# A decoder layer in fp32 on one core: last stage's second and third part in a written order, the up projection's products in a new order, and changed seams

## The chip, the cores and the metric

The kernel runs on one core of a Trainium2 chip. The metric is the device time of one execution in microseconds, the median of several runs. The engines are named as in the profile: PE (TensorE matmul), PEld (its weight load), DVE (VectorE), ACT (ScalarE), POOL (GpSimd) and SP (SyncE, which issues nearly all DMAs). L184 is line 184 of the kernel before.

## The reference

One decoder layer on x (1024 tokens, 1024 features, float32), with 256 memory tokens:

```python
h = rmsnorm(x, ln1);  z = h @ w_in              # mLSTM and attention inputs, and gates
ml_out = mlstm(...)                             # 4 heads of 128, chunkwise, normed and gated
fx_out = forgetting_attention(...)              # 8 heads of 64, causal, with decay
x = x + concat([ml_out, fx_out]) @ w_out
x = x + cross_attention(rmsnorm(x, ln_x), rmsnorm(mem, ln_mem), w_xq, w_xkv, w_xo)
u = relu(rmsnorm(x, ln2) @ w_ff1)               # 1024 -> 4096
x = x + (u * u) @ w_ff2                         # 4096 -> 1024
return rmsnorm(x, ln_f)
```

## The kernel before

Activations lie feature by token: 128 features on the partitions, eight such tiles (KT), and two halves of 512 tokens (TH). A float32 product is done as three products of rounded parts: `split` (L129 to L136) makes the rounded part `hi` on ACT and the remainder `lo` on DVE, and `mm3` (L182 to L186) issues lo x hi, hi x lo and hi x hi into one PSUM bank. TensorE thus runs on operands that ACT and DVE have to cut beforehand.

The stages in the order of the span: loading and cutting of x and the values' weights with the first products (0 to 50 us), the mLSTM projections and heads (to 380), forgetting attention (to 600), output projection `out_proj` (to 700), cross attention (to 885), the up projection (to 1215), the down projection (to 1510) and the last eighth of it with the final norm (to 1548).

What runs first on an engine is chosen by a scheduler that works on the recorded instructions, except inside `with in_order()`, where each compute engine keeps the order in which the instructions were written. DMAs from SP go in the order of SP's queue, and a DMA that has to wait holds those behind it.

PSUM has eight banks under five names (sc 3, tp 2, mm 1, m2 1, ov 1). A tile of a name can be written again once its earlier contents have been read. SBUF tiles rotate in the same way; `w2("d")` has two buffers, `rotate("d", "e")` alternates over two names with two buffers each.

*Start.* SP loads `vec` (gains, biases), then for each k a piece of x and of the weights, and at k = 2 the gate weights. `cut_w`, `cut_x`, `cut_gates` make the parts; the first matmul needs one of each.

*Memory.* `mem_prepare` loads the memory tokens, sums their squares, and cuts them to DRAM; it is issued after the first stage's last sum.

*Forgetting attention.* `Tile` scores a block of 128 queries against its keys in pieces of up to 512 columns (`parts`); a last piece narrower than 256 is computed 256 wide.

*Output projection.* `out_unit` adds one tile of the product to x for its first part, with x loaded into `rotate("p", "a")`; `full_sink` (L1071) completes it, cuts it for the cross attention and adds its square to `acc`; `row_second` turns the sums into factors.

*Up projection.* The 4096 hidden features are made in 16 pairs, each a 2x2 block product in the Winograd form of Strassen: seven products (jobs) of 12 matmuls instead of eight. Three PSUM banks hold a pair: a takes jobs 1 and 2, c takes 5 and 3, b takes 6, 7 and 4. Between two jobs on a bank the first result has to be read: `p1` (job 1) is copied by ACT, jobs 5 and 6 are added to it by DVE (`add`, L1326), and the final blocks are squared by ACT (`squared`). `jobs` sets the order:

```python
        jobs += [(p_, 1)] + ([(p_ - 1, 4)] if p_ > 2 else []) + [(p_, i) for i in (5, 2, 6, 3, 7)]
```

`left_up` cuts the weights of a pair in three groups, some additions on POOL. `put` cuts a block of the result and stores both parts to DRAM (`right`), from where the down projection loads them; `put_right` returns the steps that combine and store a pair's blocks, one of which is taken ahead of each job. `stretch` multiplies one piece of the residual by the norm's row: load, multiplication and store.

*Last stage.* The rest of the down projection (four k) comes in three parts of columns: 512 tokens of the first half, then 256 and 256 of the second. For each of eight tiles n: 12 matmuls into a bank, DVE adds the residual (L1579), ACT squares it and DVE adds the squares, ACT scales by the gain (L1584). `finish` makes the row of factors: sums by matmuls (L232), `rsqrt_cols` (DVE, POOL's pow at L202, three times DVE), `spread` (L211) of the factors over the partitions into a bank, a copy to `row` (L1558), and then four multiplications by it on DVE (L1563) with a store each (L1564). For the last part DVE reads the factors from the bank. The steps of a part's `finish` are taken between the tiles of the next part.

Of the kernel before, what the change touches and what calls it, by code (L numbers as in the profile page):

```python
# [44 lines left out]
def hybrid_layer(ctx: ExitStack, tc: tile.TileContext, a: dict, out: bass.AP):  # L45
# [146 lines left out]
    def rsqrt_cols(out_, sums, scale, n, over=None):  # L192

        var = col("var", n)
        if over is None:
            v.tensor_scalar(out=var, in0=sums, scalar1=scale, scalar2=EPS, op0=ALU.mult, op1=ALU.add)
        else:
            e = col("t", n)
            v.scalar_tensor_tensor(out=e, in0=over, scalar=EPS, in1=over, op0=ALU.mult, op1=ALU.mult)
            v.scalar_tensor_tensor(out=var, in0=sums, scalar=scale, in1=e, op0=ALU.mult, op1=ALU.add)  # L200
        y = col("y", n)
        g.tensor_tensor(out=y, in0=var, in1=half[:, :n], op=ALU.pow)  # L202
        t = col("t", n)
        v.tensor_tensor(out=t, in0=y, in1=y, op=ALU.mult)
        v.scalar_tensor_tensor(out=t, in0=t, scalar=-0.5, in1=var, op0=ALU.mult, op1=ALU.mult)
        v.scalar_tensor_tensor(out=out_, in0=t, scalar=1.5, in1=y, op0=ALU.add, op1=ALU.mult)

# [18 lines left out]
    def rsqrt_sums(acc, r, nt, parts=1, bank=None, over=None):  # L226

        ps = (bank or ov_)()
        for t in range(nt):
            for e in range(parts):  # L230
                at = (e * nt + t) * P
                nc.tensor.matmul(ps[:, t : t + 1], acc[:, at : at + P], ones, start=e == 0, stop=e == parts - 1)  # L232
        rsqrt_cols(r, ps[:, :nt], 1.0 / D, nt, over)

    def rsqrt_row(acc, r, nt, parts=1, bank=None, over=None):

        rsqrt_sums(acc, r, nt, parts, bank, over)
        rb = (bank or ov_)()
        spread(rb, r, nt)
        return rb[:, : nt * P]  # L240
# [29 lines left out]
    load(vec, a["vec"])  # L270
# [9 lines left out]
    def mem_prepare():  # L280
        acc = w2("b")
        for i in range(KT // 2):
            raw = w2("f")
            load(raw.rearrange("p (k c) -> p k c", k=2), a["mem"][:, 2 * i : 2 * i + 2])
            square_sum(acc, raw, i == 0)
            hi = w2("p", dt=F32R)
            for e in range(2):
                c = slice(e * NM, e * NM + NM)
                gain = vec[:, VEC["ln_mem"] + 2 * i + e :][:, 0:1]
                split(hi[:, c], raw[:, c].bitcast(F32R), raw[:, c], gain)  # L290
            for p_, t in enumerate((hi.bitcast(F32), raw)):
                load(hmd[:, p_, 2 * i : 2 * i + 2], t.rearrange("p (k c) -> p k c", k=2))
        rsqrt_sums(acc, rcol_m, 2, 2)
        to_row(row_m, rcol_m, 2, rowd[1:2, :NM])

# [41 lines left out]
    def cut_x(hf, k):  # L337
        split(h[hf][0][:, k], h[hf][1][:, k], xs[hf][k], vec[:, VEC["ln1"] + k :][:, 0:1])
# [168 lines left out]
    def carried(hd, y):  # L507
# [6 lines left out]
        kt = mm()  # L514
# [155 lines left out]
    with tc.issue_after(last_sum.ins):  # L670
        mem_prepare()
# [391 lines left out]
    for hf in range(2):  # L1063
# [3 lines left out]
        def full_sink(n, hf, ps):  # L1067
# [9 lines left out]
            square_sum(acc, t, n == 0, add=g)  # L1077
            if hf == 1 and n == KT - 3:
                mix_done.append(done)
            if hf and n == 2:  # L1080
                row_second(0, acc0)

        def row_second(hf, acc):
            c = rcol[:, 4 * hf : 4 * hf + 4]
            rsqrt_sums(acc, c, 4)
            at = slice(hf * TH, hf * TH + TH)
            to_row(row[:, at], c, 4, rowd[2:3, at])
# [97 lines left out]
    def left_up(p_, group):  # L1185
# [6 lines left out]
        split(hi, lo, (r1, r2, r1)[group])  # L1192
        if group == 0:
# [4 lines left out]
            by = g if p_ > 1 else v  # L1198
            by.tensor_tensor(out=x21, in0=x21, in1=x22, op=ALU.add)
            sub(x22, x21, x11, by)  # L1200
            sub(x12, x12, x22, by)
            sub(x11, h22.bitcast(F32), x22, by)
            by.tensor_tensor(out=x11, in0=x11, in1=l22.bitcast(F32), op=ALU.add)
        for e in range(2):
            cuts[p_, ((1, 2), (5, 6), (7, 3))[group][e]] = both((hi, lo), lambda t: t[:, e * TH : e * TH + TH].rearrange("p (k c) -> p k c", k=4))
# [3 lines left out]
    raws = {}  # L1209
# [4 lines left out]
    for p_ in range(2, NP - 2):  # L1214
# [54 lines left out]
    for hf in range(2):  # L1269
        oh, ol = act(), act()  # L1270
        for hd in range(XH):
# [7 lines left out]
            if hd == hf == 0:  # L1279
                row_second(1, acc0)  # L1280
# [36 lines left out]

    class Pair:


        def __init__(self, p_):
            self.p_ = p_
            self.u = {}
# [4 lines left out]
        def run(self, i, l):  # L1328
# [8 lines left out]
            if i == 1:  # L1337
                self.p1 = w2("p") if 1 < self.p_ < NP - 2 else row[:, TH * (self.p_ % 2) :][:, :TH]
# [4 lines left out]
            elif i == 5:  # L1343
                t = w4()
                u["22"], self.t1 = t[:, :TH], t[:, TH:]
# [16 lines left out]
    def put(dst, x):  # L1362

        hi = rotate("d", "e").bitcast(F32R)
# [4 lines left out]
    def put_right(b, k, pair):  # L1369

        u11, u12, u21, u22 = (pair.u[c] for c in ("11", "12", "21", "22"))
        t1 = pair.t1
        to = lambda c: [right[b][ORDER.index(c), :, p_, k] for p_ in range(2)]
        t = {}
# [12 lines left out]
        def four():  # L1387
            sub(t[4], t[2], u21)
            put(to("22"), u22)

        return [one, two, lambda: put(to("t3"), u12), four, lambda: put(to("21"), u21), lambda: put(to("t2"), t[2]), lambda: put(to("t4"), t[4])]
# [40 lines left out]

    pairs = {}
    later = []
    for at, (p_, i) in enumerate(jobs):
# [14 lines left out]
        if later:  # L1450
            later.pop(0)()
        pair = pairs.setdefault(p_, Pair(p_))
        pair.run(i, cuts.pop((p_, i)))
        if i == 4:
            b, k = todo[p_][:2]
            later += put_right(b, k, pair) if b < NB - 1 else put_plain(k, pair)
# [96 lines left out]
    def finish(acc, hf, c0, wid, parts, last):  # L1553

        rb = rsqrt_row(acc, col("r", wid // P), wid // P, parts, bank, inv[:, 4 * hf + c0 // P :][:, : wid // P])
        if not last:
            at_ = row[:, hf * TH + c0 : hf * TH + c0 + wid]
            s.activation(at_, rb, AF.Copy)  # L1558
            rb = at_
        yield  # L1560
        for k in range(0, KT, 2):
            y = x2[k // 4][:, k // 2 % 2, :, hf, c0 : c0 + wid]
            v.tensor_tensor(out=y, in0=y, in1=rb.rearrange("p (o c) -> p o c", o=1).broadcast_to([P, 2, wid]), op=ALU.mult)  # L1563
# [4 lines left out]
    for hf, c0, c1 in ((0, 0, TH), (1, 0, 256), (1, 256, TH)):  # L1568
        wid = c1 - c0
        parts = 1 if wid == TH else 2  # L1570
        acc = w2("b")
        for n in range(KT):
            if n // 2 not in w:
                last_weights(n // 2)
            ps = bank()[:, :wid]
# [3 lines left out]
            v.tensor_tensor(out=y, in0=ps, in1=y, op=ALU.add)  # L1579
            if n == KT - 1 and parts == 2:  # L1580
                s.activation(acc[:, wid:], y, AF.Square)
# [3 lines left out]
            if n:  # L1585
                next(ending, None)
        ending = finish(acc, hf, c0, wid, parts, c1 == TH and hf)
    for _ in ending:
        pass
# [54 lines left out]
```

## Time and profile before

| | us |
|---|---|
| median of 3 runs (1546.37 to 1550.0) | 1548.31 |
| profiled execution, its own time | 1549.03 |
| its span | 1547.3 |
| PE busy | 1510.3 |
| DVE busy | 1100.9 |
| ACT busy | 718.8 |
| POOL busy | 483.4 |

The span is the time from the first to the last instruction of the profiled execution; some 1.7 us lie around it. Busy times are sums over instructions. Matmuls overlap in the pipeline, so one of 512 columns shows about 0.39 us although the next starts 0.23 us after it. A wait in the profile is the idle time of an engine ahead of an instruction, put down to the instruction that released it last.

### The profile page before, as it was taken

The page shows a single profiled execution, that of the slowest core. Times are in us where ns is not written, and L with a number is a line of the kernel's source. Part 1 is how long each engine was busy: PE and PEld are TensorE (multiplying, and loading weights), DVE is VectorE, ACT ScalarE, POOL GpSimd, SP SyncE. Part 2 cuts the span into 40 slices and gives each one's busy share as a digit, 9 for nine tenths or more (in the row PEclk, how much of TensorE's full clock was granted, in tenths as well). Part 3 has the DMA queues.
Part 4 walks back from the last instruction along what each step waited for, and adds up shares of the span by engine and source line. Part 5 has one row for each costly group of instructions (what it writes and reads, how often), then busy time and mean ns, then how long its engine had stood idle before and what let it go on. Part 6 is the DMA issues. An engine that isn't in the chain of part 4 may idle for free.

```text
span 1547.3 us, 21934 instructions
## 1 busy us (share of the span) xinstructions
PE 1510.3 (98%) x7729; PEld 1261.5 (82%) x7729; DVE 1100.9 (71%) x1722; ACT 718.8 (46%) x1337; POOL 483.4 (31%) x515
## 2 busy tenths in 40 slices
PE   8999999999999999999999999999999999999997
PEld 8878888889898887788888788777778778888887
DVE  7656676665788874854457987777777787777766
ACT  7324343334678763543344456555455532222234
POOL 0002130413455441511110034453444644433310
PEclk9999999999999999999999999999999999999998
DMA  6422223436887948953344446776776965556623
GB/s 220 122 79 82 100 100 114 130 130 162 253 248 219 305 166 286 327 176 124 122 147 153 150 148 230 268 253 230 250 243 219 370 251 217 219 207 227 236 92 110
DMA packets 118075, 297.25 MB, mean 192 GB/s; under 512 B 13118, under 2 KB 27768, under 8 KB 111820
## 3 DMA queue, kind: packets, MB, share of 16 engines
q1 hardware_dynamic: 117964, 295.84, 55.9%
q8 instruction: 61, 1.00, 0.3%
q14 instruction: 50, 0.41, 0.1%
HBM read 199.08 MB, written 96.71 MB: 191 GB/s over the span
## 4 chain that ended last, share of the span: by engine, by line
PE 82%; DMA 7%; DVE 6%; issue 2%; ACT 2%; POOL 0%; SPq 0%; DVEq 0%; POOLq 0%; ACTq 0%
PE tp L184 7%; PE tp L186 7%; PE tp L185 7%; PE mm L184 5%; PE sc L184 5%; PE sc L186 5%; PE sc L185 5%; PE mm L186 5%; PE mm L185 5%; PE m L184 5%; PE m L186 5%; PE m L185 5%; PE ov L184 2%; PE ov L185 2%; PE ov L186 2%
## 5 line engine op out<-in xcount | busy, mean ns | idle before, releaser
L184 PE MATMUL tp<-act,wl 128*128 128x512 f32 (+1 forms) x448 | 176.1, 394 | 4.8 <-DVE r_f L1326 3.4
L185 PE MATMUL tp<-act,wh 128*128 128x512 f32 (+1 forms) x448 | 175.3, 391 | 0.0
L186 PE MATMUL tp<-act,wh 128*128 128x512 f32 (+1 forms) x448 | 174.9, 392 | 0.0
L133 DVE TENSOR_TENSOR wl<-wr,wh 128x1024 fp32r<-128x1024 f32 (+2 forms) x99 | 126.3, 1276 | 26.7 <-ACT wh L132 26.3
L132 ACT ACTIVATE wh<-wr 128x1024 fp32r<-128x1024 f32 (+2 forms) x99 | 99.0, 1000 | 94.5 <-PE tp L186 32.7
L184 PE MATMUL mm<-act,wl 128*128 128x512 f32 (+1 forms) x336 | 130.6, 389 | 3.5 <-DVE r_e L1071 1.3
L186 PE MATMUL mm<-act,wh 128*128 128x512 f32 (+1 forms) x336 | 129.0, 384 | 0.0
L185 PE MATMUL mm<-act,wh 128*128 128x512 f32 (+1 forms) x336 | 128.8, 383 | 0.0
L184 PE MATMUL m<-act,wl 128*128 128x512 f32 (+1 forms) x312 | 120.3, 386 | 0.9 <-DVE r_a L916 0.9
L186 PE MATMUL m<-act,wh 128*128 128x512 f32 (+1 forms) x312 | 119.3, 382 | 0.0
L185 PE MATMUL m<-act,wh 128*128 128x512 f32 (+1 forms) x312 | 119.1, 382 | 0.0
L184 PEld LDWEIGHTS tp<-act,wl 128*128 128x128 f32 x448 | 84.2, 188 | 25.4 <-DVE r_f L1326 3.8
L184 PE MATMUL sc<-act,wl 128*128 128x512 f32 (+1 forms) x252 | 98.7, 392 | 3.8 <-DVE r_f L1326 2.3
L1410 POOL TENSOR_TENSOR z<-wr 128x256 f32<-128x256 f32 x56 | 53.5, 976 | 150.4 <-DMA wr<-w_ff2q 127.9
L186 PEld LDWEIGHTS tp<-act,wh 128*128 128x128 f32 x448 | 84.2, 188 | 19.2
L185 PEld LDWEIGHTS tp<-act,wh 128*128 128x128 f32 x448 | 84.2, 188 | 18.8
L185 PE MATMUL sc<-act,wh 128*128 128x512 f32 (+1 forms) x252 | 98.4, 390 | 0.0
L186 PE MATMUL sc<-act,wh 128*128 128x512 f32 (+1 forms) x252 | 98.3, 391 | 0.0
L132 ACT ACTIVATE w<-wr 128x768 fp32r<-128x768 f32 (+2 forms) x31 | 25.5, 824 | 127.3 <-PE tp L186 70.3
L132 ACT ACTIVATE wh<-z 128x1024 fp32r<-128x1024 f32 (+1 forms) x54 | 55.5, 1027 | 61.1 <-POOL z L1410 27.3
L133 DVE TENSOR_TENSOR wl<-z,wh 128x1024 fp32r<-128x1024 f32 (+1 forms) x54 | 73.1, 1353 | 12.4 <-ACT wh L132 12.3
L184 PEld LDWEIGHTS mm<-act,wl 128*128 128x128 f32 x336 | 63.3, 188 | 17.2 <-DVE wl L133 2.1
(676 smaller groups left out, 4236.8 us busy)
## 6 DMA issues: line engine op xcount, KB each, us to landing
act<-right SPq DMA_DIRECT2D x35, 1024.0 KB
right<-w SPq DMA_DIRECT2D x56, 256.0 KB
wr<-w_ff2q SPq DMA_DIRECT2D x28, 512.0 KB
act<-fqk SPq DMA_DIRECT2D x48, 256.0 KB
wr<-w_in SPq DMA_DIRECT2D x20, 512.0 KB
wr<-w_ff SPq DMA_DIRECT2D x20, 512.0 KB
right<-r_e SPq DMA_DIRECT2D x35, 256.0 KB
right<-r_d SPq DMA_DIRECT2D x35, 256.0 KB
```

Source lines behind the costliest of these rows:

```text
L132: s.activation(hi, src, AF.Copy)
L133: return v.tensor_tensor(out=lo, in0=src, in1=hi.bitcast(F32), op=ALU.subtract)
L184: nc.tensor.matmul(ps, w[1], x[0], start=first, stop=False, skip_group_check=more)
L185: nc.tensor.matmul(ps, w[0], x[1], start=False, stop=False, skip_group_check=more)
L186: nc.tensor.matmul(ps, w[0], x[0], start=False, stop=last, skip_group_check=more)
L1410: g.tensor_tensor(out=o, in0=x, in1=y, op=op)
```

## The change

The same products are computed; only score products of 640-column rows change in shape.

- Start: `vec` and the gate weights are loaded from ACT's queue after the first piece of x; the gates are cut ahead of x, and the first piece of x in two halves.
- Memory: `mem_prepare` yields between its pieces and is stepped among the mLSTM heads. The transposed keys of head 0 use bank ov.
- Forgetting attention: rows of 640 columns are scored as 384 + 256.
- Output projection: x rotates over five tags, squares are added on DVE, and sums and row transposition are two tiles apart; the second half's follow after heads 0 and 1 of the cross attention.
- Up projection: the jobs come as 1, 5, 6, 2, (4 of the pair before), 3, 7. The third group of weights keeps one sum in a buffer of its own and is cut in two halves. `put` uses the two buffers of "d" alone. Storing is spread over a pair (four steps after job 7, three after job 4). `stretch` loads at one job and multiplies one job later, and then pauses for six.
- Last stage: parts 2 and 3 are inside `in_order()`; `finish` is divided into sums, refinement and spreading, its banks are always ov, and the products' banks rotate over the other seven; the factors are read from PSUM, but for the last part, which also copies them to `row` for POOL's multiplication; the squares of tiles 1 to 5 are added on POOL.

```diff
-        if k == 2:
-            load(wg_raw, a["w_gate"])
...
         load_x(0, k)
+        if k == 0:
+            s.dma_start(vec, a["vec"])
+            s.dma_start(wg_raw, a["w_gate"])
...
-            cut_x(0, k)
             if k in (0, 2, 4):
                 cut_gates(k // 2)
+            cut_x(0, k, 1 if k else 2)
...
-        kt = mm()
+        kt = mm() if hd else ov_()
...
-    with tc.issue_after(last_sum.ins):
-        mem_prepare()
+    closing = mem_prepare()
...
-            self.parts = [(c0, min(c0 + TH, self.wid)) for c0 in range(0, self.wid, TH)]
+            step = 384 if self.wid == 640 else TH
+            self.parts = [(c0, min(c0 + step, self.wid)) for c0 in range(0, self.wid, step)]
...
-            x = rotate("p", "a")
+            x = rotate("p", "b", "a", "p", "b")
...
-            square_sum(acc, t, n == 0, add=g)
+            square_sum(acc, t, n == 0)
...
-        split(hi, lo, (r1, r2, r1)[group])
+        if group < 2:
+            split(hi, lo, (r1, r2)[group])
+        else:
+            for c, x in ((slice(0, TH), x12), (slice(TH, 2 * TH), thirds.pop(p_))):
+                split(hi[:, c], lo[:, c], x)
...
+            s3 = thirds[p_] = w2("e") if p_ > 1 else x11
+            sub(s3, x11, x21, by)
             by.tensor_tensor(out=x21, in0=x21, in1=x22, op=ALU.add)
-            sub(x22, x21, x11, by)
+            sub(x22, x22, s3, by)
             sub(x12, x12, x22, by)
-            sub(x11, h22.bitcast(F32), x22, by)
-            by.tensor_tensor(out=x11, in0=x11, in1=l22.bitcast(F32), op=ALU.add)
...
-        jobs += [(p_, 1)] + ([(p_ - 1, 4)] if p_ > 2 else []) + [(p_, i) for i in (5, 2, 6, 3, 7)]
-    jobs += [(NP - 2, 1), (NP - 3, 4)] + both_of(NP - 2)[1:]
+        jobs += [(p_, i) for i in (1, 5, 6, 2)] + ([(p_ - 1, 4)] if p_ > 2 else []) + [(p_, 3), (p_, 7)]
+    jobs += [(NP - 1, 1), (NP - 1, 6), (NP - 2, 4)] + [(NP - 1, i) for i in (5, 7, 2, 3, 4)]
...
-        hi = rotate("d", "e").bitcast(F32R)
+        hi = w2("d", dt=F32R)
...
-        return [one, two, lambda: put(to("t3"), u12), four, lambda: put(to("21"), u21), lambda: put(to("t2"), t[2]), lambda: put(to("t4"), t[4])]
+        if last:
+            return [four, lambda: put(to("t2"), t[2]), lambda: put(to("t4"), t[4])]
+        return [one, two, lambda: put(to("t3"), u12), lambda: put(to("22"), u22)]
...
-        if at > 30 and at % 4 == 0 and stretches:
+        if at > 31 and at % 8 in (0, 7) and stretches:
             stretch(stretches[0])
-            if at % 8 == 4:
+            if at % 8 == 7:
                 stretches.pop(0)
...
+        nt = wid // P
+        r = col("r", nt)
+        end = rsqrt_sums(acc, r, nt, parts, ov_, inv[:, 4 * hf + c0 // P :][:, :nt], rsqrt_guess)
         yield
+        end()
+        yield
+        rb = ov_()[:, :wid]
+        spread(rb, r, nt)
+        rb2 = rb
+        if last:
+            rb2 = row[:, :wid]
+            s.activation(rb2, rb, AF.Copy)
         for k in range(0, KT, 2):
             y = x2[k // 4][:, k // 2 % 2, :, hf, c0 : c0 + wid]
-            v.tensor_tensor(out=y, in0=y, in1=rb.rearrange("p (o c) -> p o c", o=1).broadcast_to([P, 2, wid]), op=ALU.mult)
+            by, f = (g, rb2) if last and k == 2 else (v, rb)
+            by.tensor_tensor(out=y, in0=y, in1=f.rearrange("p (o c) -> p o c", o=1).broadcast_to([P, 2, wid]), op=ALU.mult)
             load(out[:, k : k + 2, hf * TH + c0 : hf * TH + c0 + wid], y)
             yield
...
-            ps = bank()[:, :wid]
+            turn[0] += 1
+            ps = ps_tile(tags[turn[0] % 7])[:, :wid]
...
+            if n > 1:
+                next(ending, None)
...
-                square_sum(acc[:, :wid], y, n == 0)
+                square_sum(acc[:, :wid], y, n == 0, add=g if at and n < 6 else v)
...
+    part(0, 0, 0, TH)
+    with in_order():
+        part(1, 1, 0, 256)
+        part(2, 1, 256, TH)
+        for _ in ending:
+            pass
```

More of the change, by code (lines that the diff above doesn't have):

```diff
@@ L189, in both, with rsqrt_guess @@
         return f(pair[0]), f(pair[1])
-    def rsqrt_cols(out_, sums, scale, n, over=None):
+    def rsqrt_guess(out_, sums, scale, n, over=None):
         var = col("var", n)
@@ L224, in square_sum, with rsqrt_sums @@
             add.tensor_tensor(out=acc, in0=sq, in1=acc, op=ALU.add)
-    def rsqrt_sums(acc, r, nt, parts=1, bank=None, over=None):
+    def rsqrt_sums(acc, r, nt, parts=1, bank=None, over=None, how=rsqrt_cols):
         ps = (bank or ov_)()
@@ L232, in rsqrt_sums @@
                 nc.tensor.matmul(ps[:, t : t + 1], acc[:, at : at + P], ones, start=e == 0, stop=e == parts - 1)
[L233 to L240, printed above, removed]
+        return how(r, ps[:, :nt], 1.0 / D, nt, over)
     rowd = dram.tile([4, T], F32, name="rowd")
@@ L335, in hybrid_layer, with cut_x @@
     tiles = [[ps_tile(t)[:, :WV] for t in ts] for ts in (("mm", "tp", "m2", "tp"), ("sc", "sc", "sc"))]
-    def cut_x(hf, k):
-        split(h[hf][0][:, k], h[hf][1][:, k], xs[hf][k], vec[:, VEC["ln1"] + k :][:, 0:1])
+    def cut_x(hf, k, n=1):
+        for c in range(0, TH, TH // n):
+            c = slice(c, c + TH // n)
+            split(h[hf][0][:, k, c], h[hf][1][:, k, c], xs[hf][k][:, c], vec[:, VEC["ln1"] + k :][:, 0:1])
     def first_values(hf, k, ts):
@@ L1449, in hybrid_layer @@
             lefts = left(a["w_ff2q"][0, 0])
-        if later:
-            later.pop(0)()
+        for _ in range(2 if len(later) > 5 else 1):
+            if later:
+                later.pop(0)()
         pair = pairs.setdefault(p_, Pair(p_))
         pair.run(i, cuts.pop((p_, i)))
+        b, k = todo[p_][:2]
+        if i in (7, 4) and b < NB - 1:
+            later += put_right(b, k, pair, i == 4)
+        elif i == 4:
+            later += put_plain(k, pair)
         if i == 4:
-            b, k = todo[p_][:2]
-            later += put_right(b, k, pair) if b < NB - 1 else put_plain(k, pair)
             del pairs[p_]
@@ L1567, in hybrid_layer, with part @@
     ending = iter(())
-    for hf, c0, c1 in ((0, 0, TH), (1, 0, 256), (1, 256, TH)):
+    tags = [t for t in cycle if t != "ov"]
+    def part(at, hf, c0, c1):
+        nonlocal ending
         wid = c1 - c0
-        parts = 1 if wid == TH else 2
+        parts = 2 if at else 1
         acc = w2("b")
```

66 lines of the change are left out of this document (35 added, 31 removed).

## The prediction

> **What bounds the kernel now.** I read the page's head first, then the windows by stage, then the waits of TensorE, and for each long wait the timeline around it.
>
> ```profile
> span 1547.3 us, 21934 instructions
> PE 1510.3 (98%) x7729; PEld 1261.5 (82%) x7729; DVE 1100.9 (71%) x1722; ACT 718.8 (46%) x1337; POOL 483.4 (31%) x515
> ...
> 885.00:1215.00 330.00, 318.77 (x1357) 254.34 (x1356) 255.75 (x292) 187.63 (x291) 150.47 (x96) 0.99 0.67 234
> 50.00:380.00 330.00, 329.06 (x1782) 280.69 (x1781) 213.17 (x343) 121.43 (x211) 66.36 (x81) 1.00 0.35 109
> 380.00:600.00 220.00, 216.78 (x1435) 188.93 (x1434) 173.29 (x416) 154.84 (x422) 98.98 (x156) 1.00 0.78 242
> 600.00:700.00 100.00, 96.28 (x459) 78.40 (x457) 64.26 (x82) 46.45 (x80) 30.93 (x24) 1.00 0.73 254
> 1215.00:1510.00 295.00, 294.79 (x1265) 237.25 (x1264) 218.99 (x284) 79.63 (x92) 113.41 (x116) 1.00 0.57 219
> ```
>
> The columns of a window after its length are busy us of PE, PEld, DVE, ACT and POOL. TensorE is busy for 1510.3 of 1547.3 us. The change removes no product, so all it can win, apart from some narrower score products below, is among the 37 us in which TensorE stands still. They are not spread evenly: 330.00 - 318.77 = 11.2 us lie in the up projection (885 to 1215), 3.7 in the output projection (600 to 700), 3.2 in the forgetting attention (380 to 600), 0.2 in the down projection, and most of the rest at the start, at the seam of the first stages, and at the end. What TensorE waited for says which edits can reach them:
>
> ```profile
> PE mm L184 <- DVE wl L133: 8.3, 3, 7.1
> PE tp L184 <- DVE r_f L1326: 3.4, 1, 3.4
> PE mm L211 <- DVE c_r L206: 2.9, 1, 2.9
> PE sc L184 <- DVE r_f L1326: 2.3, 1, 2.3
> PE ov L184 <- DVE r_f L1326: 2.2, 1, 2.2
> PE sc L184 <- DVE wl L133: 1.4, 1, 1.4
> PE mm L184 <- DVE r_e L1071: 1.3, 1, 1.3
> PE mm L184 <- DVE r_c L518: 0.9, 1, 0.9
> ...
> PE m L184 <- DVE act L136: 0.8, 1, 0.8
> ```
>
> The numbers are us in total, times, longest. L1326 is the addition that empties a bank in the up projection; the three waits for it make 7.9 of the 11.2 us there.
>
> **Up projection.** The timeline around the longest of them (start, duration):
>
> ```profile
> 996.66 0.40 PE L185 MATMUL m<-act,wh 128*128 128x512 f32 x1
> 996.89 0.39 PE L186 MATMUL m<-act,wh 128*128 128x512 f32 x1
> 1000.65 0.50 PE L184 MATMUL tp<-act,wl 128*128 128x512 f32 x1 [3.37 <-DVE r_f L1326]
> ...
> 994.26 1.23 DVE L1430 TENSOR_TENSOR w<-w,row 128x1024 f32<-128x1024 f32 x1 [1.55 <-DMA w<-x2d]
> ...
> 998.70 0.69 DVE L133 TENSOR_TENSOR r_p<-r_p,r_d 128x512 fp32r<-128x512 f32 x1
> ...
> 999.91 0.69 DVE L1326 TENSOR_TENSOR r_f<-tp,r_p 128x512 f32<-128x512 f32 x1
> ```
>
> Matmuls of 512 columns issue 0.23 us apart, so a job of 12 is 2.8 us. Bank b takes job 6, is read by the addition, then takes jobs 7 and 4. In the old order 1, 4 (of the pair before), 5, 2, 6, 3, 7 one job lies between 6 and 7, and one between 7 and 4: VectorE has 2.8 us to get to the addition. Here its queue was late by 1.55 us at the multiplication by the row, which waited for its load, and the addition began at 999.91. In the new order 1, 5, 6, 2, 4, 3, 7 the built program has three jobs between 6 and 7, four between 7 and 4 and two between 1 and 2, the shortest: no wait on a bank nearer than 25 matmuls after the first pairs, 5.8 us. The largest lateness seen, 2.8 + 3.37 us, would exceed that by 0.4. So the 7.9 us go. The load for the row's multiplication gets over two jobs instead of standing directly ahead of it, and the waits on wl (1.4, and 1.0 of the 8.3 above) come 25 instead of 23 matmuls after their cause; I count them as gone, -2.4. The remaining 0.9 us, at the first pairs, stay. POOL and VectorE do one operation fewer per pair for the third group; POOL, with 150 of 330 us busy, is no bound, nor is VectorE with 256.
>
> Against it stands the new `put`, which has two buffers for the first half instead of four:
>
> ```profile
> 968.10 6.67 DMA right<-r_e
> ...
> 1014.50 3.20 DMA right<-r_d
> ...
> 95.25 0.63 ACT L132 ACTIVATE r_d<-r_c 128x512 fp32r<-128x512 f32 x1 [4.38 <-DVE r_c L518]
> ```
>
> ScalarE now waits for a store to land, and behind that in its queue stand the activations and the copy of job 1's bank. I leave 1.0 us for it: -7.9 - 2.4 + 1.0 = **-9.3** (from -5.2, half of what goes, to -10.3).
>
> **Start.** Rows of the first 7 us:
>
> ```profile
> 0.79 0.40 SPq L270 DMA_DIRECT2D vec<-vec  x1
> ...
> 5.42 0.72 ACT L135 ACTIVATE act<-act,vec 128x512 fp32r<-128x512 f32 x1 [0.40 <-DMA act<-x]
> 6.17 0.75 DVE L136 SCALAR_TENSOR_TENSOR act<-act,vec,act 128x512 fp32r<-128x512 f32 x1 [0.69 <-ACT act L135]
> 6.48 0.24 ACT L132 ACTIVATE wh<-z 128x48 fp32r<-128x48 f32 x1 [0.34 <-DMA z<-w_gate]
> ```
>
> The vector and the gate weights go to ScalarE's queue, so SP's first weight load leaves 0.4 us earlier, and the first split is cut into halves: the first matmul waits for half of 0.72 + 0.75, another 0.7 less. The gate's split now stands ahead of it, and its landing, 6.48 in the old order, must come forward with its issue; where it doesn't, only some 0.4 is won. Take **-1.0** (-0.4 to -1.4).
>
> **Seams of the first stages.** The memory's squares and splits leave the stretch at 44 to 47 us, where they stood in ScalarE's queue ahead of the values' split that TensorE waited for 0.8 us; they are issued in steps among the mLSTM heads, where TensorE loses 0.9 of 330 us and VectorE is busy 213: that hides them, with their loads, the stores on SP, two sums and a transposition; without that cover they would cost the same 0.8. Head 0's transposed keys go to bank ov, so that the next product no longer waits for their reading (0.9). Sum -1.7 at best; **-1.6** (0 to -1.7).
>
> **Forgetting attention.** Rows of 640 columns are scored as 384 + 256 instead of 512 + 128, where 128 was computed 256 wide: 16 products (8 heads by 2) lose 128 columns, 16 x 0.23 / 4 = -0.9. Of the 3.2 us of stalls around them 0.6 may go with the smaller first piece: **-1.5** (-0.3 to -2.9).
>
> **Output projection.** A rotation of five tags for x instead of two, squares added on VectorE instead of POOL, and the factors' sum and transposition two tiles apart. The waits on L1071 (1.3) and on the other half's addition stand in the 3.7 us; the wait on `r_d` stays at 14 matmuls, as short as before. **-2.0** (+0.5 to -3.5): VectorE, 64 of 100 us busy, takes the additions.
>
> **The end.** Start, duration of the last steps:
>
> ```profile
> 1534.68 0.28 PE L186 MATMUL ov<-act,w 128*128 128x256 f32 x1
> ...
> 1535.44 0.38 ACT L1558 ACTIVATE row<-mm 128x256 f32<-128x256 f32 x1 [0.39 <-PE mm L211]
> ...
> 1535.86 2.50 DVE L1563 TENSOR_TENSOR act<-act,row 128x512 f32<-128x512 f32 x4 [0.44 <-ACT row L1558]
> ...
> 1536.18 0.83 PE L232 MATMUL sc<-ones,r_b 128*128 128x1 f32 x6 [0.66 <-ACT r_b L1581]
> 1538.27 0.16 DVE L200 SCALAR_TENSOR_TENSOR c_var<-sc,c_t 128x2 f32<-128x2 f32 x1
> ...
> 1539.94 1.19 PE L211 MATMUL mm<-ident,c_r 128*128 128x128 f32 x4 [2.93 <-DVE c_r L206]
> 1541.17 2.48 DVE L1563 TENSOR_TENSOR act<-act,mm 128x512 f32<-128x512 f32 x4 [1.38 <-PE mm L211]
> 1541.93 2.12 SPq L1564 DMA_DIRECT2D out<-act  x4
> ...
> L1503 POOL TENSOR_TENSOR act<-act 128x512 f32<-128x512 f32 x12 | 18.1, 1519 | 18.1 <-DVE act L1530 18.0
> ```
>
> The sums ended at 1536.18 + 0.83 = 1537.0, 2.3 us after the last product, but four multiplications of part 2 (2.50 us) kept VectorE from the variance until 1538.27, 3.6 after it. In the written order part 2's scaling is stepped while part 3's products run, and the copy of its row (0.38) no longer stands ahead of the last square; the sums get bank ov only when part 2's last reading is done, for which I add 0.1: variance at 2.3 - 0.4 + 0.1 = 2.05, 1.5 us earlier. Behind the spread matmuls, which ended at 1541.13, it gives some back. Four multiplications of 0.62 ended 2.5 us after that, each with a store behind it. Now the factors are first copied to `row` (0.4), and POOL takes the second multiplication, 1.52 us where VectorE takes 0.62; SP issues the stores in order, 0.53 each, so that two wait behind POOL's: 0.4 + 1.5 + 2 x 0.53 = 3.0 to the last issue. Net -1.5 + 0.5 = **-1.0** (+0.5 to -1.5). [...]
>
> **Sum.** -9.3 - 1.0 - 1.6 - 1.5 - 2.0 - 1.0 = -16.4. The profiled execution took 1549.03 us (span 1547.3 and 1.7 around it); 1549.03 - 16.4 = 1532.6. It lies 0.7 above the median of the runs shown, 1548.31, so the median after is forecast at 1532.
>
> **Rivals.** *Half of the up projection only.* VectorE still works in bursts: the addition at 999.91 was preceded by four of its own operations without a gap, and the new order brings jobs 5 and 6, both of which end in additions to the same copy of job 1, next to each other. If stalls come back at the new places for half the gain, -5.2 stands for -9.3, and the median is 1536; with the smaller terms at their weak ends (-0.4, 0, -0.3, +0.5, +0.5) 1543. For it: 7.9 us sat on three places only, so bursts decide. Against: 25 matmuls are double the old room. 0.20.
>
> *Stores hold ScalarE (slower).* Place: the copy of job 1's bank, which stands behind the first-half copies of `put`. From the end of the job whose result is stored: addition 0.69, three activations of 0.63 and issue make 2.9; landing 3.20 gives 6.1; seven activations of 0.63 to the end of the copy give 10.5. The built order needs the copy 61 matmuls after that job, 14.2 us. So 3.6 us are spare, and a landing of 6.8 uses them up; one of 6.67 was seen. It turns the sign when the mean lateness in the 12 pairs that store this way exceeds 16.4 / 12 = 1.4 us, at landings of 8.2; at 9.2, 12 x 2.4 - 16.4 = +12, some 1561. For it: SP issues in order, and its stores queue behind other waits. Against: the window moves 234 GB/s at a DMA share of 0.67. [...]
>
> *Nothing comes of it.* The stages outside the written order are placed by a scheduler; if its new order moves the stalls rather than removing them, and the end gives back what it wins, the time is 1548. 0.04. The forecast has 0.68.
>
> **Chances.** This kernel's measurement can tell about 0.2%, 3 us, from no change. Faster 0.68 + 0.20 = 0.88, same 0.03, slower 0.09. The range: all terms at their strong ends give -21.3, 1527, and 2 us of spread between runs, 1525; the high end is the weak case, 1543, with the same spread, 1545. The slower rival and no change lie outside.
>
> **What would show it.** In the changed profile: TensorE busy in the up projection to within 2 us of its stage, no wait there on the addition's line over 1 us; the first matmul near 6.1; no wait at 47 and 95 us; the variance 2 us after the last product and the last store's issue 3 us after the spread. The forecast is wrong if ScalarE shows waits for DMA right<-r_d in the up projection with TensorE waits on the copy of job 1 behind them, or if the row's multiplication still waits on its load.

## The result and the profile after

The changed kernel takes 1527.39 us (median of 4 runs, 1526.16 to 1528.97), the kernel before, run again beside it, 1547.58 (4 runs): a ratio of 0.9862 with a 95% interval from 0.9850 to 0.9875, or 20.2 us less. Forecast was 1532, -16.4 us. Two executions far above all others, 2484.25 us at a granted clock of 0.555 (the run with the old schedule of the row's multiplication) and 3549.69 us (the kernel before), count in no median or ratio of this text. The head of the page after, and its windows, cut where the stages begin (columns as in the prediction: length, busy us of PE, PEld, DVE, ACT, POOL, then granted clock, DMA share, GB/s):

```profile
span 1525.5 us, 21947 instructions
PE 1504.9 (99%) x7729; PEld 1261.5 (83%) x7729; DVE 1103.9 (72%) x1740; ACT 722.6 (47%) x1353; POOL 444.7 (29%) x498
...
0.00:48.30 48.30, 41.78 (x325) 41.57 (x326) 35.50 (x73) 33.13 (x59) 5.06 (x14) 1.00 0.59 210
48.30:376.90 328.60, 328.60 (x1785) 280.94 (x1783) 213.97 (x340) 121.78 (x211) 67.64 (x79) 1.00 0.36 111
376.90:694.80 317.90, 313.26 (x1897) 268.01 (x1896) 239.75 (x517) 202.86 (x507) 105.19 (x168) 1.00 0.76 247
...
880.60:1196.10 315.50, 315.50 (x1358) 254.53 (x1357) 257.60 (x307) 191.00 (x307) 125.11 (x87) 1.00 0.68 244
1196.10:1489.60 293.50, 293.50 (x1265) 236.93 (x1264) 221.62 (x283) 76.35 (x88) 114.81 (x112) 1.00 0.58 220
1489.60:1525.50 35.90, 26.46 (x222) 25.93 (x220) 18.75 (x45) 16.12 (x35) 10.99 (x14) 0.87 0.33 118
```

The same stages of the kernel before, cut at the same matmuls:

```profile
0.00:50.00 50.00, 42.13 (x324) 41.96 (x325) 36.10 (x73) 34.53 (x62) 4.21 (x14) 1.00 0.62 214
50.00:380.40 330.40, 329.45 (x1784) 281.09 (x1783) 213.40 (x343) 121.81 (x212) 66.36 (x81) 1.00 0.35 109
380.40:700.90 320.50, 313.55 (x1895) 267.83 (x1895) 237.68 (x499) 201.41 (x502) 129.91 (x180) 1.00 0.76 245
...
886.70:1217.20 330.50, 319.27 (x1359) 254.71 (x1359) 255.26 (x292) 188.38 (x293) 150.47 (x96) 0.99 0.68 236
1217.20:1511.20 294.00, 293.79 (x1266) 236.70 (x1265) 218.47 (x284) 77.91 (x89) 113.41 (x116) 1.00 0.57 217
1511.20:1547.30 36.10, 26.34 (x222) 25.91 (x220) 22.81 (x55) 14.91 (x36) 2.52 (x3) 0.87 0.33 118
```

(The cross attention, 185.80 us in both, is left out.) The lengths of the stages give the account: 1.7 us at the start, 1.8 in the mLSTM heads, 2.6 in forgetting attention and output projection, 0 in the cross attention, 15.0 in the up projection, 0.5 in the down projection, 0.2 in the last stage. Sum 21.8, the difference of the spans. The up projection's TensorE is busy for 315.50 of 315.50 us: no idle time is left there. VectorE and ScalarE do as much as before in less time. What TensorE still waits for:

```profile
PE mm L184 <- DVE act L136: 6.5, 1, 6.5
PE ov L217 <- DVE c_r L209: 1.7, 1, 1.7
PE tp L185 <- DMA act<-mix: 1.3, 1, 1.3
PE ov L238 <- DVE c_t L199: 1.2, 1, 1.2
```

All three waits on the addition are gone, and those at 47 and 95 us. The end of the changed kernel, start and duration:

```profile
1513.56 0.28 PE L186 MATMUL tp<-act,w 128*128 128x256 f32 x1
...
1515.05 1.02 PE L238 MATMUL ov<-ones,r_b 128*128 128x1 f32 x8 [1.20 <-DVE c_t L199]
1516.11 0.16 DVE L200 SCALAR_TENSOR_TENSOR c_var<-ov,c_t 128x2 f32<-128x2 f32 x1 [1.14 <-PE ov L238]
...
1517.79 1.19 PE L217 MATMUL ov<-ident,c_r 128*128 128x128 f32 x4 [1.72 <-DVE c_r L209]
1519.01 0.38 ACT L1589 ACTIVATE row<-ov 128x256 f32<-128x256 f32 x1 [3.72 <-PE ov L217]
1519.43 1.88 DVE L1593 TENSOR_TENSOR act<-act,ov 128x512 f32<-128x512 f32 x3 [1.79 <-ACT row L1589]
1519.47 1.26 POOL L1593 TENSOR_TENSOR act<-act,row 128x512 f32<-128x512 f32 x1 [2.42 <-ACT row L1589]
...
1520.14 2.08 SPq L1594 DMA_DIRECT2D out<-act  x4
```

The variance comes 2.55 us after the last product (3.59 before), the spread begins after 4.23 (5.26). From there to the end it takes 7.70 us (7.38 before): VectorE stands 0.4 us behind ScalarE's copy.

### The profile page after: what moved, and what is told of

Read it like the earlier page. It is cut to its first block, busy times and chain, and to the rows that moved or that the text cites. A ratio compares the mean times of both kernels' runs of the same rounds, so it can differ in the third digit from the quotient of the medians.

```text
span 1525.5 us, 21947 instructions
## 1 busy us (share of the span) xinstructions
PE 1504.9 (99%) x7729; PEld 1261.5 (83%) x7729; DVE 1103.9 (72%) x1740; ACT 722.6 (47%) x1353; POOL 444.7 (29%) x498
## 4 chain that ended last, share of the span: by engine, by line
PE 94%; DMA 2%; DVE 1%; ACT 1%; issue 1%; POOL 0%; SPq 0%; DVEq 0%; ACTq 0%; POOLq 0%
PE tp L184 8%; PE tp L186 8%; PE tp L185 8%; PE sc L184 6%; PE sc L186 6%; PE sc L185 6%; PE m L184 6%; PE mm L184 6%; PE m L186 6%; PE m L185 6%; PE mm L186 6%; PE mm L185 6%; PE ov L785 2%; PE ov L184 2%; PE ov L185 2%; PE ov L186 2%
## 5 line engine op out<-in xcount | busy, mean ns | idle before, releaser
L185 PE MATMUL tp<-act,wh 128*128 128x512 f32 (+1 forms) x456 | 178.7, 392 | 1.3 <-DMA act<-mix 1.3
L184 PE MATMUL tp<-act,wl 128*128 128x512 f32 (+1 forms) x456 | 179.2, 394 | 0.6 <-DVE wl L133 0.4
L186 PE MATMUL tp<-act,wh 128*128 128x512 f32 (+1 forms) x456 | 178.4, 392 | 0.0
L132 ACT ACTIVATE wh<-wr 128x1024 fp32r<-128x1024 f32 (+3 forms) x100 | 96.1, 962 | 107.6 <-PE tp L186 36.6
L133 DVE TENSOR_TENSOR wl<-wr,wh 128x1024 fp32r<-128x1024 f32 (+3 forms) x100 | 116.9, 1170 | 21.1 <-ACT wh L132 21.0
L185 PE MATMUL mm<-act,wh 128*128 128x512 f32 (+1 forms) x332 | 126.9, 382 | 0.0
L186 PE MATMUL mm<-act,wh 128*128 128x512 f32 (+1 forms) x332 | 126.8, 382 | 0.0
L185 PEld LDWEIGHTS tp<-act,wh 128*128 128x128 f32 x456 | 85.8, 188 | 20.7 <-issue 1.6
L186 PEld LDWEIGHTS tp<-act,wh 128*128 128x128 f32 x456 | 85.8, 188 | 19.6
L185 PE MATMUL sc<-act,wh 128*128 128x512 f32 (+1 forms) x260 | 100.5, 387 | 0.0
L186 PE MATMUL sc<-act,wh 128*128 128x512 f32 (+1 forms) x260 | 100.5, 387 | 0.0
L132 ACT ACTIVATE wh<-z 128x1024 fp32r<-128x1024 f32 (+2 forms) x55 | 52.5, 956 | 64.5 <-POOL z L1428 28.3
L133 DVE TENSOR_TENSOR wl<-z,wh 128x1024 fp32r<-128x1024 f32 (+2 forms) x55 | 68.2, 1240 | 9.9 <-ACT wh L132 9.9
L186 PEld LDWEIGHTS mm<-act,wh 128*128 128x128 f32 x332 | 62.4, 188 | 12.6
```

The source lines that it names most:

```text
L132: s.activation(hi, src, AF.Copy)
L133: return v.tensor_tensor(out=lo, in0=src, in1=hi.bitcast(F32), op=ALU.subtract)
L184: nc.tensor.matmul(ps, w[1], x[0], start=first, stop=False, skip_group_check=more)
L185: nc.tensor.matmul(ps, w[0], x[1], start=False, stop=False, skip_group_check=more)
L186: nc.tensor.matmul(ps, w[0], x[0], start=False, stop=last, skip_group_check=more)
```

## The experiments

All of them are edits of the changed kernel. Stage lengths are read between the same matmuls as above: 315.5 us in the up projection of the changed kernel, 330.4 before. Where only one execution was made, its stages are read from its trace and its whole time is given, but it proves little: the times of one kernel lie 3 to 8 us apart.

**The whole up projection of before** (`left_up`, order, `Pair`, `put`, storing and the row's schedule taken over as they were):

```diff
-        jobs += [(p_, i) for i in (1, 5, 6, 2)] + ([(p_ - 1, 4)] if p_ > 2 else []) + [(p_, 3), (p_, 7)]
+        jobs += [(p_, 1)] + ([(p_ - 1, 4)] if p_ > 2 else []) + [(p_, i) for i in (5, 2, 6, 3, 7)]
-        hi = w2("d", dt=F32R)
+        hi = rotate("d", "e").bitcast(F32R)
...
```

> The changed kernel with the whole up projection of before (order of jobs, third group of weights, steps of storing, four buffers, schedule of the row's multiplication); all other edits stay. The two traces put 14.9 us of the difference into this stage (330.4 against 315.5 us for the same 1357 matmuls). If the stage's gain is its own, this kernel takes 14 to 16 us more than the changed one, 1541 to 1544 us, and the stalls on the addition come back. If the gain came from what the earlier stages leave behind (other buffers, other order of loads), it stays within 5 us of the changed kernel.

1547.39 us, ratio to the kernel before 0.9995 (0.9981 to 1.0009). The up projection takes 332.1 us and the three waits on the addition are back (its line is L1334 here):

```profile
PE m L184 <- DVE r_f L1334: 3.8, 1, 3.8
PE tp L184 <- DVE r_f L1334: 2.2, 1, 2.2
PE tp L184 <- DVE wl L133: 2.1, 2, 1.7
PE sc L184 <- DVE r_f L1334: 2.0, 1, 2.0
```

The stage's gain is its own. That the median lost 20 us is more than the 14 to 16 expected: besides 16.6 in this stage, 3.8 appeared in the down projection of this trace, which has one stall of 1.9 at its beginning.

**Only the old order of the jobs** (the first pair of lines above, and the order of the last two pairs, which is written apart; nothing else):

> The changed kernel with only the order of the jobs as before: 1, 4 of the pair before, 5, 2, 6, 3, 7. Theory (distance on the banks): one job stands again between 6 and 7 and between 7 and 4, so the addition's waits return: 8 to 12 us slower than the changed kernel, 1535 to 1540 us, with waits on the addition of 2 to 4 us each. Rival (VectorE was only late because of the row's multiplication, whose load now has time): no more than 3 us slower, under 1531.

1542.44 us, 0.9964 (0.9951 to 0.9978). The up projection takes 331.9 us: the order alone is worth the whole stage, more than the 8 to 12 us of the theory and far beyond the rival's 3. But the waits on the addition, 2 to 4 us each by the theory, are three of 0.5 to 1.5, and most of the waiting names another instruction:

```profile
PE mm L184 <- DVE wl L133: 4.1, 1, 4.1
PE m L184 <- DVE wl L133: 1.7, 2, 1.2
PE tp L184 <- DVE r_f L1338: 1.5, 1, 1.5
```

In this trace VectorE works from 1172.6 us to the end of the 4.1 us stall at 1180.4 with one gap of 0.16; the remainder of the weights (wl), which TensorE waits for, stands last in that queue, behind an addition and two other cuts. That the new way of storing is what puts it last was not tested.

**Only the old schedule of the row's multiplication:**

```diff
-        if at > 31 and at % 8 in (0, 7) and stretches:
+        if at > 30 and at % 4 == 0 and stretches:
...
-            if at % 8 == 7:
+            if at % 8 == 4:
```

> The changed kernel with only the schedule of the row's multiplication as before (every fourth job a load or a multiplication). Theory (distance on the banks): VectorE waits for its load again, some 19 us in all, but TensorE hardly sees it: 0 to 2 us slower, 1527 to 1530. Rival (the late multiplication was the cause of the stalls): 6 to 12 us slower, 1533 to 1540, with TensorE waits right behind L1448.

1527.35 us (three executions), 0.9862 (0.9837 to 0.9888), up projection 315.5 us: the same. Nor did VectorE wait 19 us for the load, as I had expected. In the new order this schedule is free, and in the old order the new schedule did not help, as the run before this one shows.

**Four buffers in `put`:**

```diff
-        hi = w2("d", dt=F32R)
+        hi = rotate("d", "e").bitcast(F32R)
```

> The changed kernel with the first halves of stored blocks in four buffers again (two names in turn) instead of two; the second name is shared with the weights' third sum. ScalarE's waits on the landing of stores, 6.9 us in 7 waits in the changed kernel, should mostly go. If they cost TensorE nothing, as the profile after says, the time stays within 1 us of the changed kernel, 1526 to 1529. If two buffers cost the 1.0 us that the prediction allowed, it is about 1 us faster, at the stage's start and nowhere else, and if sharing a name with the third sum makes a new wait, up to 5 us slower.

1530.14 us, 0.9883 (0.9860 to 0.9905): 2.8 us slower than the changed kernel by the medians, though the intervals overlap. In the trace, which is of the slowest of its four executions (1532.86), the up projection takes 319.5. POOL's third sum of the weights lives in r_e and now waits for stores:

```profile
POOL r_e L1172 <- DMA right<-r_e: 21.9, 5, 5.3
...
PE m L184 <- DVE wl L133: 3.3, 2, 2.1
```

So two buffers were no price of the change: with four, nothing is won and the third sum waits. That this wait is what makes wl late is not shown; ahead of the longest wait on wl (978 us) POOL had last waited for VectorE, not for a store.

**Job 6 one job before 7, all else apart:**

```diff
-        jobs += [(p_, i) for i in (1, 5, 6, 2)] + ([(p_ - 1, 4)] if p_ > 2 else []) + [(p_, 3), (p_, 7)]
+        jobs += [(p_, 1), (p_, 5)] + ([(p_ - 1, 4)] if p_ > 2 else []) + [(p_, i) for i in (2, 6, 3, 7)]
```

> The changed kernel with the jobs in the order 1, 5, 4 (of the pair before), 2, 6, 3, 7: one job between 6 and 7 as before, all other turnarounds of a bank with at least two jobs between. In the built program four of the additions are waited for after 13 matmuls, as with the whole old order, and 18 further waits lie at 22 to 24. Theory (short distances on a bank make the stalls): the up projection takes 320 to 330 us instead of 315.5, with waits on the addition at the 13s. Rival (the old order is bad because job 4 of the pair before stands early, right behind job 1): 315 to 318.

1533.03 us, 0.9903 (0.9882 to 0.9923), up projection 320.0: 4.4 us more, at the lower end of what the theory gave and beyond the rival. But its sign, waits on the addition at the 13s, did not come: the waits are on the weights' remainder (2.3 us in all), none is on the addition.

**Job 4 early, two jobs between 6 and 7:**

```diff
-        jobs += [(p_, i) for i in (1, 5, 6, 2)] + ([(p_ - 1, 4)] if p_ > 2 else []) + [(p_, 3), (p_, 7)]
+        jobs += [(p_, 1)] + ([(p_ - 1, 4)] if p_ > 2 else []) + [(p_, i) for i in (5, 6, 2, 3, 7)]
```

> The changed kernel with the jobs in the order 1, 4 (of the pair before), 5, 6, 2, 3, 7: job 4 early as before, but two jobs between 6 and 7. In the built program no wait of the steady pairs is nearer than 24 matmuls, against 25 in the changed kernel. Theory (short distances): 315 to 318 us in the up projection, within 2 us of the changed kernel. Rival (job 4 early is what makes the stalls): 322 to 332.

1533.79 us, 0.9900 (0.9884 to 0.9916), up projection 322.1, 6.6 us more: the theory's 315 to 318 fell, and the rival's 322 to 332 was met at its low end. The waits are on the addition itself, short and often:

```profile
PE sc L184 <- DVE r_f L1338: 1.1, 2, 0.6
PE m L184 <- DVE r_f L1338: 0.8, 1, 0.8
PE ov L184 <- DVE r_f L1338: 0.7, 1, 0.7
```

One of them, VectorE's queue and the end of the stall:

```profile
1088.56 1.23 DVE L1448 TENSOR_TENSOR w<-w,row 128x1024 f32<-128x1024 f32 x1 [2.00 <-DMA w<-x2d]
1089.70 0.68 DVE L1338 TENSOR_TENSOR r_f<-m,r_p 128x512 f32<-128x512 f32 x1
...
1090.43 0.50 PE L184 MATMUL m<-act,wl 128*128 128x512 f32 x1 [0.83 <-DVE r_f L1338]
```

In the built programs, every addition of the changed kernel's steady pairs has at least 37 matmuls, three jobs or 8.6 us, until its bank is used again; only ScalarE's copy of job 1 and the weights are at 25. Here 35 additions stand at 24 to 26, and VectorE misses those 5.6 us by 0.2 to 0.8. At 13 matmuls it missed by 2.2 to 3.4 in the kernel before, but with 6 one job before 7 not at all.

So the distance is not the whole cause, and in this run it is not parted from job 4's early place, the rival's reason. The order also changes how late VectorE comes. That can be read on the banks mm, m2 and ov, of which there is one each, from the end of a job's last matmul to the end of its addition (955 to 1170 us). It is 1.1 us at the median and 2.4 at most in the changed kernel, 2.4 and 5.7 in the kernel before, 3.7 and 6.4 here. For 2.4 us, two jobs of room would have been enough. The room is used where VectorE comes late: with four buffers it was 6.0 us late at most, had three jobs, and no addition was waited for. Why VectorE comes sooner in the new order is not shown.

**The last stage as before** (no `in_order`, the old `finish`):

> The changed kernel with the last stage as before (no written order, factors copied to the row but for the last part, all multiplications on VectorE, banks from the common rotation). From the last product to the end the two traces have 12.63 us before and 11.92 after, from the stage's first tile to the last product 23.49 and 23.94. If the tail's gain is its own and small, this kernel's stage takes 35.9 to 36.3 us against 35.86, so 0.1 to 0.4 us more. If the prediction's -1.0 was right and something else in the changed kernel hid it, it takes 36.7 or more.

One execution, 1529.44 us. The last stage takes 23.36 + 12.63 = 35.99 us against 23.94 + 11.92 = 35.86. The new last stage is worth 0.13 us (the last spread takes 1.19 us in both).

**Last four multiplications on VectorE alone:**

```diff
-            by, f = (g, rb2) if last and k == 2 else (v, rb)
+            by, f = v, rb
...
-            rb2 = row[:, :wid]
-            s.activation(rb2, rb, AF.Copy)
```

> The changed kernel without POOL's share of the last four multiplications and without the copy of the factors that stands ahead of VectorE's first one. Theory (the copy of 0.38 us delays VectorE, and taking one of four multiplications away from it doesn't pay for that since the stores go in SP's order): from the spread's first matmul to the end 7.3 to 7.5 us instead of 7.70. Rival (POOL's help pays): 7.9 to 8.3, as VectorE's four multiplications take 2.5 us instead of 1.9.

```profile
1518.22 0.99 PE L217 MATMUL ov<-ident,c_r 128*128 128x128 f32 x4 [1.72 <-DVE c_r L209]
1519.25 2.48 DVE L1589 TENSOR_TENSOR act<-act,ov 128x512 f32<-128x512 f32 x4 [1.18 <-PE ov L217]
```

From the spread's first matmul to the end 7.19 us instead of 7.70, below what was expected, since the four spread matmuls took 0.99 instead of 1.19 (in the changed kernel they run at a granted clock of 0.50, which it has from 1516.16 us on). With that put back, 7.39: copy and POOL's share together cost 0.3 us. The time of one run, 1527.32, can't tell that from the changed kernel's.

**The start as before** (vector and gates from SP, x whole and ahead of the gates):

> The changed kernel with the start as before: vector and gate weights from SP, x cut whole and ahead of the gates. If the start's 0.61 us (7.07 against 6.46) are its own, the first matmul comes at 7.0 to 7.1 again, and what follows to the 324th matmul takes no less than the changed kernel's 41.8. If they come from chance in the first loads' landing, it starts within 0.2 of 6.46.

One execution, 1530.04 us. First matmul at 7.11 (6.46), and 44.3 us from there to the 324th instead of 41.8, with two new waits behind VectorE's cutting:

```profile
PE mm L184 <- ACT wh L132: 7.1, 1, 7.1
PE sc L184 <- DVE act L136: 1.2, 1, 1.2
PE mm L184 <- DVE w L375: 1.1, 1, 1.1
```

In the eleven traces in which start and memory are as changed, the 324th matmul comes at 48.2 to 49.0 us, here at 51.4. The waits of 1.2 and 1.1 us are not in the kernel before, so they are not what the new start saves against it; one of 0.5 to 0.9 us stands near 30 us in five of the eleven traces.

**Memory and head 0's keys as before:**

> The changed kernel with the memory's preparation in one piece behind the first stage's last sum, and head 0's transposed keys in the common rotation of banks. Theory (each stall has its own cause): the wait of 0.9 us behind the reading of the keys and of 0.8 us behind the values' split come back, 1.5 to 2.2 us in the stretch to the 2106th matmul, which takes 376.9 us in the changed kernel and 380.4 before. Rival (the transposed keys alone): 0.9 to 1.3.

```profile
PE sc L184 <- DVE w L371: 1.8, 1, 1.8
PE mm L184 <- DVE r_c L519: 0.9, 1, 0.9
```

44.7 us from the first to the 324th matmul (41.8) and 330.3 from there to the 2106th (328.6): 4.6 us more, against the theory's 2.2 at most; the first matmul came 0.4 earlier (one execution, 1530.45 us). Both waits are back at 46 and 96 us. The first, 1.8 us, is 1.0 longer than in the kernel before. The two make 2.7 of the 4.6; where the rest lies is not shown.

**The output projection as before:**

> The changed kernel with the output projection as before (x in two tags in turn, squares added on POOL, sums and row transposition together, the second half's behind head 0). The stretch from the 2106th to the 4000th matmul took 320.5 us before and 317.1 to 320.0 in kernels that share the changed code there. If the prediction's 2.0 are this edit's, this one takes 319.5 to 321; if not, it lies within the same 317 to 320, and the wait on the mix's load (1.3 us in the changed kernel) may be gone.

323.2 us between the 2106th and the 4000th matmul, against 315.7 to 320.0 with the changed code: 5.3 more than the changed kernel, beyond both guesses (one execution, 1532.38 us). The wait on the mix's load did not go but grew to 4.0, and behind it the granted clock is 0.50 for 6.82 us:

```profile
PE tp L184 <- DMA act<-mix: 2.3, 1, 2.3
PE tp L185 <- DMA act<-mix: 1.7, 1, 1.7
PE mm L184 <- DVE r_a L922: 1.2, 1, 1.2
...
627.64:631.05 3.41, 1.73 (x4) 0.50 1.00 337
631.05:634.46 3.41, 3.41 (x9) 0.50 0.82 319
```

The kernel before waits for no mix load and takes 320.5 us there. So this run is not its old state, and doesn't price the edit.

**Bursts on VectorE:**

```diff
             ps = getattr(self, at_)
+            if i == 1 and self.p_ in (4, 6, 8, 10, 12):
+                for _ in range(self.p_ + 4):
+                    v.memset(ps, 0.0)
```

> The changed kernel with extra work for VectorE: ahead of job 1 of pairs 4, 6, 8, 10 and 12 it writes zeros 8, 10, 12, 14 and 16 times into the bank that the job takes, 5 to 10 us each. It asks two things. First, how late VectorE may be: with two jobs (5.8 us) between every result and its bank's next use, the bursts of 5 and 6 us should cost TensorE under 1 us and those of 9 and 10 us 2 to 6 us each. Second, what a stall costs besides itself: in the kernels so far stalls of 2.1 to 4.3 us were followed four times by some 4 us at half the matmul rate (1.6 to 2.5 us more) and four times not; if length decides, those over 4 us here are all followed by it, and if not, some are not.

The scheduler spread the 60 writes (485 ns each) among the other work, so the first question has no clean answer; the up projection took 327.9 us, with stalls of 1.0, 2.6 and 4.0 us (one execution, 1540.05 us). The second is answered in the last section.

## Why the prediction was right or wrong

*Where the time goes.* Right: the gain lies in TensorE's stalls, and most of it, 14.9 of 21.8 us between the profiles, in the up projection.

*Up projection, -9.3 forecast, -14.9 measured.* That the new order takes the stalls away held; the size and the reason did not. -14.9 lies outside the term's own range (-5.2 to -10.3), and the whole stayed within its range because that range adds up the strong ends of all terms. What was mis-sized is the price of a stall, which the prediction took as its idle time: 11.2 us, of which 10.3 go. These stalls cost more. Idle is counted from the end of the last matmul, which outlasts the next issue by 0.16 us (0.39 against 0.23), and the first matmul afterwards takes 0.11 more (0.50), 0.27 for each of seven; and the stall of 2.34 at 1063 was followed by matmuls that issue up to 0.43 apart instead of 0.23, 1.5 us more. The 0.9 at the first pairs, which I let stay, went as well. That makes 11.2 + 1.9 + 1.5 = 14.6 of the 14.9. The 1.0 us allowed for ScalarE's waits on stores was not needed: it waits for them 6.9 us in all, 1.4 at the longest, and TensorE sees nothing.

The reason, room on the banks, was off in three points. Two jobs of room are not enough for an addition when VectorE comes 6 us late, as the run with job 4 early shows, and the shortest room that I counted on, 25 matmuls or 5.8 us, is less than that; the new order gives every addition three. In the changed kernel that room is hardly used, since VectorE comes 2.4 us late at most, which I did not foresee. And I read job 4 as one job behind 7 from the written list, where the scheduler places two; of the additions only those of four pairs stood at 13 or 14 matmuls.

*Start, -1.0.* 0.61 for the first matmul in this pair of traces. In the twelve traces with the changed start it comes at 6.10 to 6.62, against 7.07 and 7.11 with the old one: 0.45 to 1.0. From the first cut of x to the first matmul it takes 1.08 us instead of 1.65, 0.57 of the 0.7 counted for the split in halves. The 0.4 for the earlier issue did not come in this pair: the first cut began at 5.38 (5.42); over the twelve it began at 5.02 to 5.55.

*Seams, -1.6.* -1.15 up to the 324th matmul and -1.8 to the 2106th. The two waits, 0.8 and 0.9, are the ones named; their price was taken as bare idle time again, and with 0.27 for each they make 2.3 of these 3.0. The rest stays open. The undoing run loses 4.6, 1.0 of it in a first wait that is longer than the kernel before's.

*Attention -1.5, output projection -2.0.* Together -2.6. Cut at the 3480th matmul, near the end of the attention, it is -0.6 and -2.0. The first can't be told from chance: over the traces with the changed code this part takes 205.4 to 207.2 us, in the kernel before 207.1. The second is right in part by luck: the waits that I had named went, but of the 3.7 us of idling 1.9 are there again, 1.5 of them on the mix's load, which I had not named. The undoing run doesn't price it.

*The end, -1.0.* -0.26 (36.12 to 35.86 us), and -0.13 by the undoing run. The term that was mis-sized is "1.5 us earlier": the spread begins 1.03 earlier after the last product, because all eight sums now wait for part 2's last reading of bank ov and run 1.02 us in one piece, where two of them had run ahead. What came after the spread was near, +0.32 for +0.5. What was left out: part 2's spread, four matmuls that issue 0.11 apart and used to run in the shadow behind the last product, now stands before it, and with the rest of the new order the products end 0.45 to 0.58 later. The sum is -1.03 + 0.32 + 0.45 = -0.26. POOL's share and the copy were not worth it: without them the tail is 0.3 us shorter. POOL took 1.26 us here, 2.0 times VectorE's 0.63, where I had counted 1.52; which part of the 0.3 is the copy's and which POOL's, no run separates.

*Rivals.* Stores holding ScalarE, the rival at 0.08, did not happen. Half of the up projection did not happen, but with job 4 early it would have: 6.6 of 14.9 are lost there.

## What to carry to other kernels

With accumulation in turns on a few banks, count for every bank the matmuls between the result and the next write in the built program, and compare them with the worst lateness of the engine that reads it. Read that lateness again in the new trace, since the order changes it too. Price a stall of a busy TensorE above its idle time (14.6 us for 11.2 of idling here). When an edit is undone in a changed kernel, look whether its waits are those of the old kernel before reading a price from it. Work moved ahead of the last product is no longer free (the products end 0.45 to 0.58 us later here): look at what used to run in its shadow.

## What the runs showed of the hardware

I had not expected slow matmuls behind so short a stall. The kernel before around its longest stall (3.37 us), then around the one of 2.34 us, in windows of 3.41 us, the length of the halved clock there (columns: length, PE busy, granted clock, DMA share, GB/s):

```profile
995.48:998.90 3.42, 1.80 (x8) 1.00 0.77 298
998.90:1002.31 3.41, 1.66 (x7) 1.00 0.83 305
1002.31:1005.72 3.41, 3.41 (x17) 1.00 0.42 156
...
1060.34:1063.75 3.41, 1.07 (x5) 1.00 0.53 198
1063.75:1067.16 3.41, 3.41 (x10) 0.50 0.77 289
1067.16:1070.57 3.41, 3.41 (x16) 1.00 0.33 112
```

After the 2.34 us of idling the granted clock is 0.50 for 3.41 us and ten matmuls run in it instead of 16 or 17; after the 3.37 us it stays at 1.00, and so it does after the 2.18 us that end at 1126.25. So the length of a stall alone doesn't decide. In the windows above the 2.34 us lie in one, the 3.37 us in two, with 1.62 and 1.75 us of idling; whether that makes the difference is not shown. The 3.41 us at half the clock cost some 1.5 us: the 18 matmuls behind this stall take 5.85 us, the 18 behind the one of 2.18 us 4.30.

In the run with only the old order of the jobs, the granted clock behind the stall of 4.1 us is 0.50 from 1180.20 to 1184.00 and 0.70 on to 1188.00; in the run with the bursts, behind the stall of 4.0 us, it is 0.68 from 1121.70 to 1127.00.

At the end, with its matmuls of one column, the changed kernel has 1.29 us of idling in the 3.41 us ahead of 1516.16, from where its granted clock is 0.50. From 11 us to there it is 1.00 throughout, the output projection's stall of 1.3 us on the mix's load included; in the run with the output projection as before it is 0.50 for 6.82 us behind the waits of 2.3 and 1.7 us on that load.
